# A decoder layer on one core: eighteen seven-product blocks in the up projection in place of sixteen

## Chip, cores and metric

The kernel runs on one core of a Trainium2 chip. The metric is the device time of one execution in microseconds, the median of several runs. Beside it stands the profile of one execution, with the start and length of every instruction on the engines PE (matmul), DVE (vector), ACT (scalar), POOL and SP (here mainly a DMA queue).

## The reference, cut to what matters

The layer has a mixer (two kinds of heads), a gated MLP with a causal convolution, and a gated table lookup projection. The change touches the first product of the MLP alone:

```python
h = rms_norm(x, ffn_norm_g[i])
u = h @ w_up[i]                       # (256, 2048) @ (2048, 11264), float32
a, g = jnp.split(u, 2, axis=-1)
a = causal_dwconv(a, conv_w[i], conv_b[i])
x = x + (jax.nn.gelu(a, approximate=False) * g) @ w_down[i]
```

There are 256 tokens, that is two row halves of 128.

## The kernel before, in words

**A float32 product in three.** Every operand is split into a high part (ACT casts it, line 1219, or 286 in the earlier stages) and a low part (DVE subtracts the high part from the raw value, line 1221 or 288). One product of 128 x 128 by 128 x 512 is three matmuls (`three`, lines 353 to 355): high by high, high by low, and low by high. The first of them needs the cast of the weights alone, the second needs the subtraction too.

**Column groups.** The up projection runs over 11 column groups (`up_group(q)`, q from 0 to 10). A group takes 512 columns of `a` and 512 of `g`, and the 2048 input rows as 16 slabs of 128. Its four accumulators (two row halves by two column halves, named `up00` to `up11`) fill four PSUM banks.

**Units.** A group is a list of units, each with at most two weight slabs to load, a split (cast and subtractions) and its matmuls. A plain unit (`p`) loads one slab of 128 x 1024 values (512 KB) and makes its four products, 12 matmuls. A *seven* treats two slabs as a 2 x 2 block product and makes it with seven products, as Strassen and Winograd do: 21 matmuls where two plain units make 24. It is four units in a row (`split1`/`fn1` to `split4`/`fn4`): its first unit loads both slabs and splits half of one; the third adds halves of the slabs on DVE (lines 1666 and 1667) before its split; the fourth does so too (lines 1677 and 1678). Four of the seven products go to banks of their own (`upP1`, `upP5`, `upP6`, `upP7`), which are the four banks that the accumulators of the next group will use; after the last seven of a group they are combined into `z_up` (ACT line 1688, DVE lines 1689 to 1691).

**The order table.** `ORDERS[q]` is a string with one letter for each unit: `p` a plain unit, `a` the next quarter of the first seven, `b` of the second. A group with one seven has 18 units, one with two has 20. In the kernel before, group 0 has two; after it groups with one and with two follow in turn, and the last two groups have one each: 16 sevens.

**The turn of a group.** When a group's last slab is done, ACT takes its four accumulators out (`up_rows`, line 1077), DVE adds the `z_up` terms (line 1084, two instructions) and transposes blocks (line 191, two), and 16 small DMAs move the blocks into columns (line 197, ten on SP's queue and six on POOL's). These jobs are tied to the last unit of the group and the first of the next (`TURN_AT`). The convolution and the GELU of the group (`up_act`: ACT lines 1103, 1106 and 1113, DVE lines 1110 and 1116, split in lines 147 and 148) are tied to units 9 to 18 of the next group (`ACT_AT`, `START`). From group 2 on, DVE lines 453 to 457 and ACT line 456 make sums of the previous group's result for the down projection.

**Buffers.** The split parts live in eight buffers (`hi0` to `hi3`, `lo0` to `lo3`), two for a unit and one for the first unit of a seven; a split runs at most four units ahead (`AHEAD_UP`). The raw slabs go into eight more spaces: `raw0` to `raw2`, two in each of the tiles `u32r` and `u36r`, and one in `xs`. SP's queue issues the loads in order, and the moves of a turn stand in the same queue.

**What sets the order.** The lines above say what depends on what; a scheduler then writes one fixed list of instructions for each engine. Each engine works its list in order.

The names `part<u>_0` and `part<u>_1` are the cast and the subtraction of unit u. With the change a unit's number rises by two behind each group that gains a seven; groups, not unit numbers, are compared below.

Of the kernel before, what the change touches and what calls it, by code (L numbers as in the profile page):

```python
# [43 lines left out]

FRONT = (8, 4, 4)
SEVENS_UP = 2
ORDERS = ("pppppp" "apapapap" "bpbbbp",
          *("pppppp" "apapapap" "pppp", "ppp" "apapapap" "bpbpbpb" "pp") * 4,
          *("pppppp" "apapapap" "pppp",) * 2)
START = [sum(map(len, ORDERS[:q])) for q in range(12)]  # L50
TURN_AT = (-1, -1, 0, 0)
GATE_ORDER = "ppppp" "apapapap" "bpbpbb" "p"
# [4 lines left out]
def layer_kernel(  # L57
# [954 lines left out]
    with tc.tile_pool(name="ffn", bufs=1) as fp:  # L1012
# [609 lines left out]
        def up_group(q):  # L1622
# [3 lines left out]

            n7 = "a" in ORDERS[q], "b" in ORDERS[q]
            first, n7 = 2 * sum(n7), sum(n7)
# [81 lines left out]
            kinds = {"p": iter(us), "a": iter(seven(0)), "b": iter(seven(1))}  # L1710
            return [next(kinds[c]) for c in ORDERS[q]]

# [71 lines left out]
```

## Time and profile before

| | |
|---|---|
| median of 3 runs (lowest, highest) | 1234.77 us (1232.65, 1235.25) |
| the profiled execution's own time | 1232.94 us |
| its span, first to last instruction | 1231.2 us |
| mixer and output projection | about 0 to 430 us of the span |
| up projection, 11 groups | about 430 to 905 us |
| down projection | about 905 to 1110 us |
| gate and output | about 1110 to 1231 us |
| DMA packets of the whole span | 276.36 MB, mean 224 GB/s |

A view of groups has one row for each line, engine and shape, with the count, the busy time and the mean length of one. A view of windows has one row for each stretch, and for each engine its busy time and number of instructions. A timeline has one row for instructions that follow each other, with start, length, engine, line and count; in square brackets stands the idle time before it and what ended it. The length of an instruction is longer than the distance to the next on the same engine, since they overlap a little: distances come from the timeline, not from the mean length. "us to landing" is the time from a DMA's issue to its end.

### The profile page before, as it was taken

The page shows a single profiled execution, that of the slowest core. Times are in us where ns is not written, and L with a number is a line of the kernel's source. Part 1 is how long each engine was busy: PE and PEld are TensorE (multiplying, and loading weights), DVE is VectorE, ACT ScalarE, POOL GpSimd, SP SyncE. Part 2 cuts the span into 40 slices and gives each one's busy share as a digit, 9 for nine tenths or more (in the row PEclk, how much of TensorE's full clock was granted, in tenths as well). Part 3 has the DMA queues.
Part 4 walks back from the last instruction along what each step waited for, and adds up shares of the span by engine and source line. Part 5 has one row for each costly group of instructions (what it writes and reads, how often), then busy time and mean ns, then how long its engine had stood idle before and what let it go on. Part 6 is the DMA issues. An engine that isn't in the chain of part 4 may idle for free.

```text
span 1231.2 us, 16367 instructions
## 1 busy us (share of the span) xinstructions
PE 1224.2 (99%) x5596; PEld 1031.2 (84%) x5596; DVE 978.5 (79%) x1210; ACT 747.8 (61%) x1095; POOL 186.8 (15%) x347
## 2 busy tenths in 40 slices
PE   9999999999999999999999999999999999999998
PEld 7999988888888888888888888888888888888887
DVE  6788857665565689789998898998788998899773
ACT  7667545565554455766676676757656556556552
POOL 2011237243304201011101101110110000050000
PEclk9999999999999999999999999999999999999999
DMA  8566687676557786777687678766797896777670
GB/s 304 181 198 195 175 229 223 185 221 188 161 183 218 224 312 208 241 218 242 204 273 242 183 255 268 225 174 221 240 316 247 298 345 208 253 230 229 199 230 35
DMA packets 131301, 276.36 MB, mean 224 GB/s; under 512 B 14906, under 2 KB 24626, under 8 KB 131090
## 3 DMA queue, kind: packets, MB, share of 16 engines
q1 hardware_dynamic: 119312, 256.87, 65.6%
q0 software_dynamic: 11520, 18.29, 5.3%
q8 instruction: 44, 0.72, 0.2%
q14 instruction: 40, 0.32, 0.1%
q10 hardware_dynamic: 385, 0.16, 0.0%
HBM read 247.46 MB, written 8.93 MB: 208 GB/s over the span
## 4 chain that ended last, share of the span: by engine, by line
PE 99%; DVE 0%; DMA 0%; ACT 0%; issue 0%; SPq 0%; DVEq 0%
PE up L353 11%; PE up L355 11%; PE up L354 11%; PE tg L343 9%; PE tg L344 9%; PE tg L342 8%; PE pg L353 3%; PE pg L354 3%; PE pg L355 3%; PE dnP L1271 1%; PE dnP L1270 1%; PE upP L355 1%; PE upP L354 1%; PE upP L353 1%; PE dnP L1269 1%; PE gt L354 1%
## 5 line engine op out<-in xcount | busy, mean ns | idle before, releaser
L288 DVE TENSOR_TENSOR lo<-raw,hi 128x1024 fp32r<-128x1024 f32 (+3 forms) x130 | 153.4, 1182 | 108.3 <-ACT hi L286 108.0
L355 PE MATMUL up<-part,x2T 128*128 128x512 f32 x608 | 236.6, 389 | 0.0
L354 PE MATMUL up<-part,x2T 128*128 128x512 f32 x608 | 236.5, 389 | 0.0
L1219 ACT CAST part<-raw 128x1024 fp32r<-128x1024 f32 (+1 forms) x147 | 146.5, 1007 | 111.5 <-PE up L355 35.1
L286 ACT CAST hi<-raw 128x1024 fp32r<-128x1024 f32 (+3 forms) x130 | 132.1, 1017 | 124.1 <-PE tg L344 70.1
L1221 DVE TENSOR_TENSOR part<-raw,part 128x1024 fp32r<-128x1024 f32 (+1 forms) x141 | 163.1, 1162 | 31.6 <-ACT part L1219 25.8
L353 PE MATMUL up<-part,x2T 128*128 128x512 f32 x608 | 185.0, 389 | 0.0
L354 PEld LDWEIGHTS up<-part,x2T 128*128 128x128 f32 x608 | 114.2, 188 | 23.6
L355 PEld LDWEIGHTS up<-part,x2T 128*128 128x128 f32 x608 | 114.1, 188 | 23.6
L353 PEld LDWEIGHTS up<-part,x2T 128*128 128x128 f32 x608 | 114.2, 188 | 23.6
L344 PE MATMUL tg<-hi,hT 128*128 128x512 f32 x288 | 113.7, 396 | 0.0
L343 PE MATMUL tg<-lo,hT 128*128 128x512 f32 x288 | 113.2, 393 | 0.2 <-DVE lo L288 0.2
L342 PE MATMUL tg<-hi,hT 128*128 128x512 f32 x288 | 112.5, 397 | 0.0
L197 POOL DMA_DIRECT2D EZ<-Y x66 | 35.0, 538 | 373.2 <-issue 205.3
L1219 ACT CAST part<-u36r 128x1024 fp32r<-128x1024 f32 (+1 forms) x46 | 47.8, 1041 | 35.1 <-PE up L355 16.3
L1221 DVE TENSOR_TENSOR part<-u36r,part 128x1024 fp32r<-128x1024 f32 (+1 forms) x46 | 55.5, 1207 | 11.5 <-ACT part L1219 7.2
L343 PEld LDWEIGHTS tg<-lo,hT 128*128 128x128 f32 x288 | 54.1, 188 | 11.3 <-DVE lo L288 0.4
L344 PEld LDWEIGHTS tg<-hi,hT 128*128 128x128 f32 x288 | 54.0, 188 | 11.2 <-DVE hT L151 0.2
L342 PEld LDWEIGHTS tg<-hi,hT 128*128 128x128 f32 x288 | 53.8, 188 | 10.6
L1221 DVE TENSOR_TENSOR part<-u32r,part 128x1024 fp32r<-128x1024 f32 (+1 forms) x44 | 50.3, 1145 | 12.1 <-ACT part L1219 9.2
L1219 ACT CAST part<-u32r 128x1024 fp32r<-128x1024 f32 (+1 forms) x44 | 43.4, 991 | 21.4 <-DVE u32r L1667 7.7
L354 PE MATMUL pg<-lo,hT 128*128 128x430 f32 (+1 forms) x156 | 55.7, 357 | 0.0
(861 smaller groups left out, 2714.3 us busy)
## 6 DMA issues: line engine op xcount, KB each, us to landing
raw<-in_w_up_dram SPq DMA_DIRECT2D x78, 512.0 KB, 5.1
raw<-in_w_in_dram SPq DMA_DIRECT2D x71, 512.0 KB, 4.3
u36r<-in_w_up_dram SPq DMA_DIRECT2D x43, 512.0 KB, 5.0
raw<-in_w_down_dram SPq DMA_DIRECT2D x42, 512.0 KB, 6.0
u32r<-in_w_up_dram SPq DMA_DIRECT2D x34, 512.0 KB, 5.2
raw<-in_w_out_dram SPq DMA_DIRECT2D x32, 512.0 KB, 4.8
xs<-in_w_up_dram SPq DMA_DIRECT2D x21, 512.0 KB, 4.9
w2b<-in_w_down_dram SPq DMA_DIRECT2D x20, 512.0 KB, 6.0
```

Of the source, the lines that this page charges most:

```text
L197: (other if other and (4 * a + b) % 3 else pool).dma_start(out=c[32 * b : 32 * b + 32, a::4], in_=y[32 * a : 32 * a + 32, :, b])
L286: act.copy(hi, raw)
L288: dve.tensor_sub(lo, raw, f32(hi))
L342: pe.matmul(o, ah, hi[:, i, :], start=first, stop=False)
L343: pe.matmul(o, ah, lo[:, i, :], start=False, stop=False)
L344: pe.matmul(o, al, hi[:, i, :], start=False, stop=last)
L353: pe.matmul(o, ah, hi, start=start, stop=False)
L354: pe.matmul(o, ah, lo, start=False, stop=False)
L355: pe.matmul(o, al, hi, start=False, stop=stop)
L1219: act.copy(r32(hi), raw)
L1221: dve.tensor_sub(r32(lo), raw, hi)
L1269: pe.matmul(o, ah, hi, start=first, stop=False)
```

## The change

The order table is written with two names, one for a group with one seven and one for a group with two, and the groups behind group 0 now follow as two, two, one, three times, and one at the end.

```diff
 FRONT = (8, 4, 4)
 SEVENS_UP = 2
-ORDERS = ("pppppp" "apapapap" "bpbbbp",
-          *("pppppp" "apapapap" "pppp", "ppp" "apapapap" "bpbpbpb" "pp") * 4,
-          *("pppppp" "apapapap" "pppp",) * 2)
+ONE = "pppppp" "apapapap" "pppp"
+TWO = "ppp" "apapapap" "bpbpbpb" "pp"
+ORDERS = ("pppppp" "apapapap" "bpbbbp", TWO, TWO, ONE, TWO, TWO, ONE, TWO, TWO, ONE, ONE)
 START = [sum(map(len, ORDERS[:q])) for q in range(12)]
```

Groups 1, 5 and 7 gain a seven, and group 6 loses one. Groups 1, 2, 5 and 8 now follow a group with two sevens with two of their own; before, no group did.

**ACT at the turn from group 0 to group 1.** Unit 23 was a plain unit and is now the first quarter of a seven (with half a slab to cast), and unit 24, a plain unit, has its slab in `u32r`. Before:

```order
L1077 ACTIVATE EZ_4102<-up11_4137,rstd_ffn_4098 128x512
L1219 CAST part22_0_4439<-u36r_4095 128x1024
L1077 ACTIVATE EZ_4102<-up10_4135,rstd_ffn_4098 128x512
L1219 CAST part23_0_4462<-u32r_4094 128x1024
L1219 CAST part24_0_4501<-raw24_0_4384 128x1024
```

Now:

```order
L1077 ACTIVATE EZ_4102<-up11_4137,rstd_ffn_4098 128x512
L1219 CAST part22_0_4437<-u36r_4095 128x1024
L1219 CAST part24_0_4499<-u32r_4094 128x1024
L1077 ACTIVATE EZ_4102<-up10_4135,rstd_ffn_4098 128x512
L1219 CAST part23_0_4462<-u32r_4094 128x512
```

The cast of unit 24 has moved ahead of the last of the four evictions (line 1077) and of the cast of unit 23.

**DVE at the turn from group 4 to group 5.** Group 5 begins with unit 96 before and with unit 98 now; it has one seven before and two now. Before:

```order
L1691 TENSOR_TENSOR xs_84<-upP5_5642,xs_84 128x2x512
L1221 TENSOR_TENSOR part99_1_5863<-u32r_4094,part99_0_5862 128x1024
L455 TENSOR_TENSOR Sf_5831<-xs_84,Sf_5831 128x128
L1084 SCALAR_TENSOR_TENSOR EZ_4102<-xs_84,rstd_ffn_4098,EZ_4102 128x1024 x2
L457 TENSOR_TENSOR Sp_5832<-Sf_5831,Sp_5832 128x4x128
L191 STREAM_TRANSPOSE Y_4103<-EZ_4102 128x8x4x32 x2
L1221 TENSOR_TENSOR part100_1_5902<-u32r_4094,part100_0_5901 128x1024
```

Now:

```order
L1691 TENSOR_TENSOR xs_84<-upP5_5648,xs_84 128x2x512
L455 TENSOR_TENSOR Sf_5836<-xs_84,Sf_5836 128x128
L1221 TENSOR_TENSOR part101_0_5869<-u36r_4095,part101_0_5869 128x512
L1084 SCALAR_TENSOR_TENSOR EZ_4102<-xs_84,rstd_ffn_4098,EZ_4102 128x1024 x2
L1666 TENSOR_TENSOR u36r_4095<-u36r_4095 128x512
L457 TENSOR_TENSOR Sp_5837<-Sf_5836,Sp_5837 128x4x128
L191 STREAM_TRANSPOSE Y_4103<-EZ_4102 128x8x4x32 x2
L1667 TENSOR_TENSOR u36r_4095<-u36r_4095 128x512
L1221 TENSOR_TENSOR part102_1_5907<-raw102_0_5757,part102_0_5906 128x1024
```

A subtraction of 1024 values has become one of 512, and the two additions of a seven (lines 1666 and 1667) now stand among the turn's instructions, ahead of the next full subtraction.

**PE at the same turn.** Unit 102 is now the fourth unit of its group, and unit 105 the third quarter of its first seven. Before, where the first row shown is 38 matmuls behind the start of group 5:

```order
L355 MATMUL up11_5870<-part98_0_5839,x2T0_3674 128x512
L353 MATMUL up11_5870<-part99_0_5862,x2T0_3674 128x512
L354 MATMUL up00_5867<-part99_1_5863,x2T0_3674 128x512
L355 MATMUL up00_5867<-part99_0_5862,x2T0_3674 128x512
L354 MATMUL up01_5869<-part99_1_5863,x2T0_3674 128x512
L355 MATMUL up01_5869<-part99_0_5862,x2T0_3674 128x512
```

Now, where it is 41 behind:

```order
L355 MATMUL upP1_5946<-part101_0_5869,x2T0_3674 128x512
L353 MATMUL up11_5875<-part102_0_5906,x2T0_3674 128x512
L353 MATMUL upP5_6004<-part105_0_5950,S_up0_4092 128x512
L353 MATMUL upP7_6008<-part105_0_5950,S_up0_4092 128x512
L354 MATMUL up00_5872<-part102_1_5907,x2T0_3674 128x512
L355 MATMUL up00_5872<-part102_0_5906,x2T0_3674 128x512
```

Two matmuls of unit 105, which read its cast, now stand ahead of the matmuls of unit 102 that read its subtraction. PE's list has the same form at the turn from group 0 to group 1, where the two matmuls read `part27_0` and stand 50 matmuls behind the start of group 1 (43 at the turn shown here); at the turns from group 1 to 2 and from 7 to 8 no matmul of a later unit stands there.

## The prediction

> **What bounds the kernel now.** I read the page first, its share of busy time and its chain of waits, then the view of who waited for whom, then windows that cut the up projection at the first matmul of its groups.
>
> ```profile
> span 1231.2 us, 16367 instructions
> ...
> PE 1224.2 (99%) x5596; PEld 1031.2 (84%) x5596; DVE 978.5 (79%) x1210; ACT 747.8 (61%) x1095; POOL 186.8 (15%) x347
> ...
> PEclk9999999999999999999999999999999999999999
> ...
> PE 99%; DVE 0%; DMA 0%; ACT 0%; issue 0%; SPq 0%; DVEq 0%
> ```
>
> The chain that ended last is PE's from end to end. The view of waits, asked for PE alone, has three rows, and all of them lie in the first stage:
>
> ```profile
> PE xT L159 <- DMA xs<-in_x_dram: 1.5, 1, 1.5
> PE warm L100 <- DVE ones L96: 1.1, 1, 1.1
> PE tg L343 <- DVE lo L288: 0.2, 1, 0.2
> ```
>
> So PE never stood still in the up projection, and a matmul that is left out there is worth its full time, as long as no wait comes up. The windows below are groups 4 (two sevens), 5 (one seven) and 2 to 9 together; the columns are PE, PEld, DVE, ACT and POOL with busy time and count, then the granted clock, the share of DMA, and GB/s.
>
> ```profile
> 600.84:643.00 42.16, 42.16 (x187) 34.92 (x186) 39.22 (x44) 30.34 (x43) 3.75 (x7) 1.00 0.75 236
> 643.00:685.84 42.84, 42.84 (x190) 35.48 (x189) 36.94 (x37) 27.51 (x38) 3.77 (x7) 1.00 0.76 236
> 515.84:855.84 340.00, 340.00 (x1501) 281.63 (x1500) 304.02 (x317) 231.22 (x313) 29.41 (x55) 1.00 0.73 228
> ```
>
> The last row gives PE's pace: 340.00 / 1501 = 0.2265 us for a matmul of 128x512. The first two give the worth of a seven: 42.84 - 42.16 = 0.68 us, three matmuls. They show its price too: DVE is busy for 39.22 of 42.16 us in a group with two sevens, and for 36.94 of 42.84 with one. A group of two has some 3 us to spare on DVE, and these are not spread evenly: at the turn of a group a run of evictions and transposes stands in DVE's list.
>
> **What goes away.** Three groups gain a seven and one loses one, two more in all, six matmuls fewer: 6 x 0.2265 = **-1.36 us**. The loads stay (a seven reads the slabs of two plain units). DVE and ACT get more work, but over the eight groups in the last window DVE is busy for 304.02 of 340 us, so what two sevens add is hidden in sum. What counts are the four turns at which a group of two now follows a group of two: 0 to 1, 1 to 2, 4 to 5 and 7 to 8.
>
> **The turn from group 4 to 5.** Up to here DVE's list is unchanged in kind, so the trace can be used with its own clock. Group 5 starts at 643.00, and this is the turn on DVE, on ACT and on PE (three answers of the timeline):
>
> ```profile
> 644.12 1.22 DVE L1691 TENSOR_TENSOR xs<-upP,xs 128x1024 f32<-128x1024 f32 x1
> 645.25 1.22 DVE L1221 TENSOR_TENSOR part<-u32r,part 128x1024 fp32r<-128x1024 f32 x1
> 646.38 0.28 DVE L455 TENSOR_TENSOR Sf<-xs,Sf 128x128 f32<-128x128 f32 x1
> 646.59 2.48 DVE L1084 SCALAR_TENSOR_TENSOR EZ<-xs,rstd_ffn,EZ 128x1024 f32<-128x1024 f32 x2
> 648.98 0.68 DVE L457 TENSOR_TENSOR Sp<-Sf,Sp 128x512 fp32r<-128x512 f32 x1
> 649.58 2.37 DVE L191 STREAM_TRANSPOSE Y<-EZ 128x1024 f32<-128x1024 f32 x2
> 651.87 1.18 DVE L1221 TENSOR_TENSOR part<-u32r,part 128x1024 fp32r<-128x1024 f32 x1
> ```
>
> ```profile
> 641.84 2.42 ACT L1077 ACTIVATE EZ<-up,rstd_ffn 128x512 f32<-128x512 f32 x4 [0.30 <-PE up L355]
> ...
> 650.72 1.05 ACT L1219 CAST part<-u32r 128x1024 fp32r<-128x1024 f32 x1 [3.40 <-DMA u32r<-in_w_up_dram]
> ```
>
> ```profile
> 643.00 0.39 PE L353 MATMUL up<-part,x2T 128*128 128x512 f32 x1
> ...
> 652.75 0.39 PE L355 MATMUL up<-part,x2T 128*128 128x512 f32 x1
> ```
>
> DVE has no idle time in it. From start to start an instruction of 1024 values takes 1.13 us (644.12 to 645.25), one of 512 takes 0.60 (648.98 to 649.58), the pair of line 1084 2.39 and that of line 191 2.29. In the new list the subtraction of 1024 is one of 512, and the additions of the seven come in, line 1666 ahead of the transposes and line 1667 behind them. From 645.25 on: 0.21 (L455) + 0.60 (subtraction) + 2.39 + 0.60 (L1666) + 0.60 (L457) + 2.29 = 651.94, so line 1667 ends at 651.94 + 0.68 = 652.62. Only then can ACT cast the third quarter of the seven, unit 105: 1.05 us (the ACT row), with 0.08 for the hand-overs, 653.8. In PE's list two matmuls that read this cast stand 43 matmuls behind the start of the group: 643.00 + 43 x 0.2265 = 652.74. **PE waits 1.1 us there.** The subtraction of unit 102, next on DVE, ends at 652.54 + 1.22 = 653.76, ahead of its matmul two places on, so it adds nothing. Everything behind these two matmuls waits with them.
>
> A PE that let a ready matmul pass a waiting one could take four matmuls of units 103 and 104 that read casts alone, 4 x 0.2265 = 0.9 us, and would wait only 0.2 here. The Trainium skill says that it does not (TensorE: Matmul & The Clock Gate, Step-by-step: what each phase is for): only weight loads are pulled ahead, and matmuls stay in program order. By that rule the 1.1 us stand; by the other the sum below would be 0.9 us less at each of two turns. No row here shows a waiting matmul in the up projection, so none can tell.
>
> **The turn from group 0 to 1.** Here the same form stands in PE's list, 50 matmuls behind the start of group 1, and something comes on top. The rows are those of DVE and ACT, the first matmul of group 1, SP's queue, and from the page the loads into `u32r` with their median time to landing:
>
> ```profile
> 474.98 1.22 DVE L1691 TENSOR_TENSOR xs<-upP,xs 128x1024 f32<-128x1024 f32 x1
> 476.11 1.22 DVE L1221 TENSOR_TENSOR part<-u32r,part 128x1024 fp32r<-128x1024 f32 x1
> 477.24 2.47 DVE L1084 SCALAR_TENSOR_TENSOR EZ<-xs,rstd_ffn,EZ 128x1024 f32<-128x1024 f32 x2
> 479.63 2.36 DVE L191 STREAM_TRANSPOSE Y<-EZ 128x1024 f32<-128x1024 f32 x2
> 481.92 1.18 DVE L1221 TENSOR_TENSOR part<-raw,part 128x1024 fp32r<-128x1024 f32 x1
> ```
>
> ```profile
> 472.75 1.05 ACT L1219 CAST part<-u36r 128x1024 fp32r<-128x1024 f32 x1
> 473.71 0.68 ACT L1077 ACTIVATE EZ<-up,rstd_ffn 128x512 f32<-128x512 f32 x1
> 474.28 1.04 ACT L1219 CAST part<-u32r 128x1024 fp32r<-128x1024 f32 x1
> ```
>
> ```profile
> 471.41 0.39 PE L353 MATMUL up<-part,x2T 128*128 128x512 f32 x1
> ```
>
> ```profile
> 469.92 0.54 SPq L1196 DMA_DIRECT2D u32r<-in_w_up_dram  x1
> ...
> 482.02 6.53 SPq L197 DMA_DIRECT2D EZ<-Y  x10
> 488.65 0.60 SPq L1196 DMA_DIRECT2D raw<-in_w_up_dram  x1
> ```
>
> ```profile
> u32r<-in_w_up_dram SPq DMA_DIRECT2D x34, 512.0 KB, 5.2
> ```
>
> With everything at hand DVE would run 476.11 + 0.60 (subtraction of 512) + 2.39 + 0.60 + 2.29 = 481.99, line 1667 would end at 482.68 and the cast of unit 27 at 483.8; PE needs it at 471.41 + 50 x 0.2265 = 482.74: 1.1 us again. But ACT's list now has the cast of unit 24 ahead of the last eviction (line 1077). Its slab goes to the space that this load at 469.92 fills, and by the median of its kind lands 5.2 us later, at 475.1. Behind the waiting cast stand that eviction and the cast of unit 23, and for these waits DVE: cast from 475.1, eviction from 476.1, cast of unit 23 from 476.6 to 477.3 (steps of 0.96 and 0.57 from the ACT rows, 0.6 for the half). DVE's subtraction starts at 477.3, not at 476.1, and all behind it moves by 1.2. **PE waits 2.3 us.** If the slab is early the wait is 1.1; if the scheduler's lists hide both, nothing. I take 2.3.
>
> **The other two turns.** At 1 to 2 no matmul is pulled ahead in this way. PE needs the subtraction of unit 44, 43 matmuls (9.74 us) behind the start of group 2. Ahead of it stand neither lines 455 and 457 nor line 1667: from the start of line 1691 it ends 1.13 + 2.39 + 0.60 + 2.29 + 0.60 + 1.22 = 8.23 later. If that line starts 1.12 behind the group's start, as at 643.00, the end is at 9.35, 0.4 ahead of need. At 7 to 8 line 1667 stands behind two more subtractions, and the same count comes out 0.8 ahead. I take 0 for both; the bounds are -0 and 1.1 each, the size found at 4 to 5.
>
> **The sum.** -1.36 + 1.1 + 2.3 + 0 + 0 = **+2.0 us**. The profiled execution took 1232.94 us (span 1231.2 and 1.7 around it), so it would take 1234.9. It lies 1.83 below the median 1234.77 of three runs whose spread is 2.6, so against that median: **1236.8 us**, +0.16%.
>
> **Rivals.**
>
> *A: the waits are covered.* Buffers or a shorter landing let ACT and DVE be a microsecond earlier, and PE does not wait: 1234.77 - 1.36 = 1233.4. For it: none of PE's waits lies in the up projection now. Against: DVE's seven rows at 644.12 have no gap, so there is nothing to gain there.
>
> *B: all four turns wait.* The margins of 0.4 and 0.8 at 1 to 2 and 7 to 8 are smaller than one DVE instruction. If DVE comes to line 1691 one instruction (1.13 us) late, PE waits there as well. This decides once DVE's spare time in a group of two, 42.16 - 39.22 = 2.9 us, is used up by the group before. Price: 1.1 each, +4.2 in sum, 1239.0: slower.
>
> *C: slabs late behind the moves.* The ten moves of a turn hold SP's queue (6.53 us at 482.02), and in a group of two that follows one of two the slab of its 13th unit is the first behind them, where before it was the 15th. At group 1 it would be issued at 488.7 and land 5.2 later, at 493.9; cast and subtraction (1.05 and 1.22) end at 496.2, and PE needs the subtraction 119 matmuls behind the group's start, at 498.4. A landing takes 2.2 us more than the median to be felt; then 1 us at each of four turns: 1240.8.
>
> *D: the clock falls.* A wait of 2.3 us is longer than any now (the longest is the 1.5 above, and the page's clock row stays at 9s). Were PE to run at half pace for as long as such a turn lasts, 643.00 to 652.75, that costs 9.75 / 2 = 4.9 us: 1241.7. The Trainium skill (TensorE: Matmul & The Clock Gate, What you observe and What's actually happening) puts the idle window at about 3.4 us, so by the Trainium skill a dip would cost about 1.7 us, an estimate, and a wait of 2.3 would not set it off by itself.
>
> **Chances.** The sum above 0.48, A 0.17, B 0.24, C 0.05, D 0.03, something unnamed 0.03. The likeliest alone gives 1235.4 to 1238.0 (2.3 or 1.1 at the first turn, 0.8 to 1.4 at the other). The range for 8 in 10 goes from just below A to above B: 1233.2 to 1240.5. A measurement here tells some 0.2%, 2.5 us, from no change. Faster by more than that: all six matmuls give but 0.11%, so only the unnamed, 0.03. Slower: B, C, D and the upper quarter of the likeliest, 0.32 + 0.13 = 0.45. The same: 0.52.
>
> **What would show it.** PE's waits should have rows with line 353 in the up projection: about 2 us at one place near 483 us, about 1 us near 655, released by ACT's cast (line 1219), and nothing else over 0.5 us. Six matmuls fewer on PE. On ACT a cast from `u32r` that waited for its DMA near 475. If there is no PE row at all, A is right; if rows near 525 and 780 as well, B; a release by a DMA, C; a granted clock under 1.00 in a group, D. The forecast is wrong as a whole if the time went into the down projection, where this page sees no change.

## The result, and the profile after

The changed kernel is slower: 1239.40 us in the median of 5 runs (1238.97 to 1239.44) against 1234.65 for the kernel before on the same chip (5 runs), a ratio of 1.0048 (95% interval 1.0037 to 1.0059), or 4.75 us. The forecast was 2.0. The profiled execution took 1238.97 us. From the page, span, PE's busy time and the granted clock in 40 slices:

```profile
span 1237.3 us, 16366 instructions
...
PE 1226.4 (99%) x5590; PEld 1030.9 (83%) x5590; DVE 986.5 (80%) x1222; ACT 751.1 (61%) x1099; POOL 186.8 (15%) x347
...
PEclk9999999999999999999999999999999999999999
```

Six matmuls are gone (5596 to 5590), and yet PE is busy for 2.2 us more: at a full-speed pace it would be 1.36 less. Where the time went is told by the first and the last matmul of the up projection, in the timelines of the kernel before and of the changed one:

```profile
429.91 0.39 PE L353 MATMUL up<-part,x2T 128*128 128x512 f32 x1
...
898.45 0.39 PE L355 MATMUL up<-part,x2T 128*128 128x512 f32 x1
```

```profile
429.93 0.39 PE L353 MATMUL up<-part,x2T 128*128 128x512 f32 x1
...
904.48 0.39 PE L355 MATMUL up<-part,x2T 128*128 128x512 f32 x1
```

Between them lie 468.54 us before and 474.55 now, 6.01 more; what comes ahead and behind is the same to 0.02. This length, free of what happens in the first stage, is the measure for most of what follows. PE's waits now have rows in the up projection (engine, line, what it waited for; total, times, longest):

```profile
PE upP L353 <- ACT part L1219: 3.3, 2, 2.1
...
PE up L353 <- ACT part L1219: 0.4, 1, 0.4
PE up L354 <- DVE part L1221: 0.4, 1, 0.4
```

These are four places. In PE's timeline a row in brackets gives the wait, and the distance of two rows the pace:

```profile
482.54 0.39 PE L353 MATMUL up<-part,x2T 128*128 128x512 f32 x1
485.02 0.73 PE L353 MATMUL upP<-part,S_up 128*128 128x512 f32 x2 [2.09 <-ACT part L1219]
...
486.18 0.63 PE L354 MATMUL up<-part,x2T 128*128 128x512 f32 x1
486.61 0.63 PE L355 MATMUL up<-part,x2T 128*128 128x512 f32 x1
...
655.90 0.39 PE L353 MATMUL up<-part,x2T 128*128 128x512 f32 x1
657.46 0.73 PE L353 MATMUL upP<-part,S_up 128*128 128x512 f32 x2 [1.17 <-ACT part L1219]
...
785.35 0.50 PE L354 MATMUL up<-part,x2T 128*128 128x512 f32 x1 [0.43 <-DVE part L1221]
...
893.32 1.20 PE L353 MATMUL up<-part,x2T 128*128 128x512 f32 x4 [0.44 <-ACT part L1219]
```

The first two are the waits at the turns 0 to 1 and 4 to 5. The third is at the turn 7 to 8, the fourth in the last group. Behind the first wait the matmuls stand 0.43 us apart (486.18 to 486.61) where 0.2265 is normal, and the window from there to 489.3 (columns PE, PEld, DVE, ACT, POOL, granted clock, share of DMA, GB/s) has the clock at 0.60:

```profile
485.00:489.30 4.30, 4.28 (x12) 3.38 (x13) 3.98 (x4) 0.28 (x1) 2.12 (x5) 0.60 0.73 186
```

Twelve matmuls in 4.28 us at 0.2265 would be 2.72: the low clock cost some 1.6 us of this execution.

**What the engines behind PE did.** DVE and ACT at the turn 0 to 1 of the changed kernel:

```profile
477.29 0.69 DVE L1221 TENSOR_TENSOR part<-u32r,part 128x512 fp32r<-128x512 f32 x1 [1.08 <-ACT part L1219]
477.90 2.48 DVE L1084 SCALAR_TENSOR_TENSOR EZ<-xs,rstd_ffn,EZ 128x1024 f32<-128x1024 f32 x2
480.29 0.68 DVE L1666 TENSOR_TENSOR u32r<-u32r 128x512 f32<-128x512 f32 x1
480.89 2.37 DVE L191 STREAM_TRANSPOSE Y<-EZ 128x1024 f32<-128x1024 f32 x2
483.18 0.65 DVE L1667 TENSOR_TENSOR u32r<-raw,u32r 128x512 f32<-128x512 f32 x1
```

```profile
475.12 1.05 ACT L1219 CAST part<-u32r 128x1024 fp32r<-128x1024 f32 x1 [1.30 <-DMA u32r<-in_w_up_dram]
...
483.92 1.04 ACT L1219 CAST part<-u32r 128x1024 fp32r<-128x1024 f32 x1 [1.22 <-DVE u32r L1667]
```

This is the predicted chain: the slab of unit 24 lands at 475.1, its cast holds up the eviction and the cast of unit 23, DVE stands for 1.08, line 1667 ends behind the transposes at 483.8, ACT casts, and PE starts when the cast ends. At the turn 4 to 5, DVE's and ACT's rows are these:

```profile
649.14 0.69 DVE L1221 TENSOR_TENSOR part<-u36r,part 128x512 fp32r<-128x512 f32 x1 [0.21 <-ACT part L1219]
...
655.63 0.65 DVE L1667 TENSOR_TENSOR u36r<-u36r 128x512 f32<-128x512 f32 x1
```

```profile
656.37 1.04 ACT L1219 CAST part<-u36r 128x1024 fp32r<-128x1024 f32 x1 [0.30 <-DVE u36r L1667]
```

At the turn 7 to 8 PE waits for the subtraction of unit 160, a plain unit:

```profile
776.08 1.22 DVE L1691 TENSOR_TENSOR xs<-upP,xs 128x1024 f32<-128x1024 f32 x1
777.21 1.22 DVE L148 TENSOR_TENSOR uC<-xs,uC 128x1024 fp32r<-128x1024 f32 x1
...
784.07 1.23 DVE L1221 TENSOR_TENSOR part<-u36r,part 128x1024 fp32r<-128x1024 f32 x1
```

And in the last group it waits for the cast of unit 208. ACT's list has the cast of unit 209 (from `xs`) ahead of it, with two sets of lines 1103 and 1106 around that:

```profile
887.73 1.05 ACT L1219 CAST part<-raw 128x1024 fp32r<-128x1024 f32 x1 [2.23 <-DMA raw<-in_w_up_dram]
...
889.99 1.05 ACT L1219 CAST part<-xs 128x1024 fp32r<-128x1024 f32 x1
...
892.23 1.04 ACT L1219 CAST part<-raw 128x1024 fp32r<-128x1024 f32 x1
```

### The profile page after: what moved, and what is told of

Read it like the earlier page. It is cut to its first block, busy times and chain, and to the rows that moved or that the text cites. A ratio compares the mean times of both kernels' runs of the same rounds, so it can differ in the third digit from the quotient of the medians.

```text
span 1237.3 us, 16366 instructions
## 1 busy us (share of the span) xinstructions
PE 1226.4 (99%) x5590; PEld 1030.9 (83%) x5590; DVE 986.5 (80%) x1222; ACT 751.1 (61%) x1099; POOL 186.8 (15%) x347
## 4 chain that ended last, share of the span: by engine, by line
PE 97%; DVE 1%; DMA 1%; ACT 1%; issue 0%; SPq 0%; DVEq 0%; ACTq 0%
PE up L354 11%; PE up L355 11%; PE up L353 11%; PE tg L343 8%; PE tg L342 8%; PE tg L344 8%; PE pg L353 3%; PE pg L354 3%; PE pg L355 3%; PE upP L353 1%; PE upP L355 1%; PE upP L354 1%; PE dnP L1270 1%; PE dnP L1269 1%; PE dnP L1271 1%; PE gt L353 1%
## 5 line engine op out<-in xcount | busy, mean ns | idle before, releaser
L354 PE MATMUL up<-part,x2T 128*128 128x512 f32 x596 | 232.9, 391 | 0.5 <-DVE part L1221 0.4
L355 PE MATMUL up<-part,x2T 128*128 128x512 f32 x596 | 232.9, 391 | 0.0
L353 PE MATMUL up<-part,x2T 128*128 128x512 f32 x596 | 181.8, 390 | 0.4 <-ACT part L1219 0.4
L354 PEld LDWEIGHTS up<-part,x2T 128*128 128x128 f32 x596 | 112.2, 188 | 24.6 <-DVE part L1221 1.4
L353 PEld LDWEIGHTS up<-part,x2T 128*128 128x128 f32 x596 | 112.0, 188 | 24.1 <-ACT part L1219 0.9
L355 PEld LDWEIGHTS up<-part,x2T 128*128 128x128 f32 x596 | 112.3, 188 | 23.4
L1219 ACT CAST part<-u36r 128x1024 fp32r<-128x1024 f32 (+1 forms) x51 | 51.0, 1000 | 35.6 <-PE up L354 9.8
L1221 DVE TENSOR_TENSOR part<-u36r,part 128x1024 fp32r<-128x1024 f32 (+1 forms) x51 | 59.0, 1159 | 15.6 <-ACT part L1219 10.9
```

Of the source, the lines that this page charges most:

```text
L353: pe.matmul(o, ah, hi, start=start, stop=False)
L354: pe.matmul(o, ah, lo, start=False, stop=False)
L355: pe.matmul(o, al, hi, start=False, stop=stop)
L1219: act.copy(r32(hi), raw)
L1221: dve.tensor_sub(r32(lo), raw, hi)
```

## The experiments

The time is the difference of the medians against the kernel before on the same chip, with the interval of the ratio; the length is that of the up projection in the profiled execution, less 468.54; the gaps are PE's waits in it of 0.2 us and more, by their place. (In the run with group 9 earlier one matmul of the down projection stands within that length; its 0.23 is taken off.)

| run | sevens | median, us | ratio, 95% | length | gaps at (us): size |
|---|---|---|---|---|---|
| changed kernel | 18 | +4.75 | 1.0037 to 1.0059 | +6.01 | 485: 2.09, 657: 1.17, 785: 0.43, 893: 0.44 |
| changed kernel, again | 18 | +4.71 | 1.0022 to 1.0047 | +4.29 | 486: 1.99, 657: 1.17, 785: 0.43, 893: 0.42 |
| changed kernel, third | 18 | +4.96 | 1.0023 to 1.0047 | +4.79 | 486: 1.98, 657: 1.18, 785: 0.43, 893: 0.64 |
| second seven in group 1 alone | 17 | +2.67 | 1.0008 to 1.0026 | +1.79 | 486: 2.05 |
| one seven in group 1 | 17 | +3.74 | 1.0020 to 1.0046 | +3.11 | 655: 1.17, 783: 0.43, 891: 0.97 |
| group 1 later | 18 | +3.48 | 1.0017 to 1.0040 | +3.54 | 526: 0.74, 655: 1.63, 783: 0.42, 891: 0.56 |
| group 5 earlier | 17 | +1.79 | 1.0010 to 1.0027 | +1.61 | 783: 0.43, 891: 0.20 |
| group 1 earlier | 18 | +3.13 | 1.0018 to 1.0036 | +3.57 | 484: 0.71, 655: 1.63, 784: 1.17 |
| best places, one in group 7 | 18 | +3.65 | 1.0018 to 1.0041 | +3.83 | 527: 0.73, 657: 0.27, 725: 0.37, 893: 0.64 |
| best places, groups as changed | 18 | +0.89 | 1.0000 to 1.0017 | +1.55 | 525: 0.73, 655: 0.28 |
| transposes four units later | 18 | +5.17 | 1.0030 to 1.0055 | +5.25 | 527: 1.22, 700: 1.13, 829: 1.13, 892: 0.26 |
| transposes twice at 0 to 1 | 18 | +6.05 | 1.0035 to 1.0060 | +6.04 | 486: 2.56, 530: 1.51, 658: 0.42, 787: 1.63 |
| transposes later, other groups | 18 | +6.84 | 1.0041 to 1.0068 | +7.14 | 527: 1.22, 572: 1.74, 617: 1.13, 746: 1.13 |
| the same, nineteen | 19 | +12.89 | 1.0093 to 1.0120 | +12.77 | 506: 0.20, 527: 1.23, 571: 1.74, 616: 1.74, 640: 0.21, 660: 0.70, 680: 0.79, 706: 1.75, 752: 1.13 |
| group 9 earlier | 18 | +3.84 | 1.0020 to 1.0045 | +3.99 | 485: 1.98, 656: 1.17, 784: 0.43, 847: 0.29 |
| waits taken off, eighteen | 18 | +2.93 | 1.0013 to 1.0032 | +3.25 | 526: 1.51, 680: 0.35, 808: 0.46 |
| waits taken off, seventeen | 17 | +0.82 | 0.9998 to 1.0016 | +0.55 | 636: 0.24 |

The two columns agree within 0.9 us, but for the first row (1.3), whose profiled execution has the low clock. So what these orders cost lies in the up projection, and PE's waits are nearly all of it.

**Half of the change at a time.** The first run has the kernel before with the second seven of group 1 alone, the second has the rest of the change:

```diff
-ORDERS = (..., TWO, TWO, ONE, TWO, TWO, ONE, TWO, TWO, ONE, ONE)
+ORDERS = (..., TWO, TWO, ONE, TWO, ONE, TWO, ONE, TWO, ONE, ONE)
```

> Seventeen sevens: the second seven of group 1 alone is added to the kernel before, so that only the turns 0 to 1 and 1 to 2 have two sevens on both sides. Theory (wait, then half clock): the wait of the changed kernel at 485 stays (its step is 2.48 us where 0.23 is normal: 2.25 more), and behind it the matmuls run at half pace for some 3.8 us as there (1.7 more); minus three matmuls, 0.68: the span is 3.3 us above the kernel before. Rival 1 (the low clock belongs to the whole of the change, not to this wait): the wait alone, 1.6 above, with no steps over 0.3 us behind it. Rival 2 (the waits of about 0.5 us in the last group are set by the number of sevens ahead): they are here at half their size. No wait near 528, the turn 1 to 2.

```diff
+ORDERS = (..., ONE, TWO, ONE, TWO, TWO, ONE, TWO, TWO, ONE, ONE)
```

> Seventeen sevens, with one seven in group 1: the other three gains and losses of the change stay. Theory: no wait near 485 and the clock is 1.00 in every window of the up projection; the wait at the turn 4 to 5 stays (1.4 us with its restart), that at 7 to 8 too (0.7), minus 0.68, so 1.4 us above the kernel before, and up to 2.3 if the small waits of the last group stay as well. Rival (the half clock comes with the turn of a group, whatever its wait): a window with a clock under 0.8 behind 655 too, 3 us above.

The wait at the turn 0 to 1 came alone, 2.05 us, with no low clock behind it: the length is 1.79 above, and 1.64 of it is the wait with its restart (2.32, see the account below) less the 0.68 of one seven. So the step that a gap of two microseconds brings the half clock fell at once (rival 1 gave 1.6). Rival 2 of the first run, the last group, is at zero rather than at half. The other half has the waits at 655 and 783 as in the changed kernel, and a larger one, 0.97, in the last group.

**The first seven of a group earlier or later.** `LATE` has four plain units ahead of the first seven and one behind the second, `EARLY` two and three, where `TWO` has three and two.

```diff
+LATE = "pppp" "apapapap" "bpbpbpb" "p"; EARLY = "pp" "apapapap" "bpbpbpb" "ppp"
+ORDERS = (..., LATE, TWO, ONE, TWO, TWO, ONE, TWO, TWO, ONE, ONE)
```

> The changed kernel with the first seven of group 1 one plain unit later (four plain units ahead of it, and one behind the second seven): nine matmuls, 2.04 us. Theory: the wait at 485 falls from 2.1 us to between 0 and 0.4, and the half pace behind it goes with it (1.7): 3.5 to 3.9 us below the changed kernel, some 1 us above the kernel before. Rival 1 (the half clock has another cause at that place, such as the loads or the moves): the clock still falls near 485, and only 2 us are saved. Rival 2 (with one plain unit behind the second seven, its sums are late at the next turn): a new wait near 528 of 1 to 2 us gives half of it back.

```diff
+ORDERS = (..., ONE, TWO, ONE, TWO, EARLY, ONE, TWO, TWO, ONE, ONE)
```

> As the run with one seven in group 1, and in group 5 the first seven one plain unit earlier, behind two: PE is at it nine matmuls, 2.04 us, sooner. Theory: the wait at the turn 4 to 5 grows from a gap of 1.2 us to 3.2, and now the clock falls to half behind it, as behind the gap of 2.1 at 485 of the changed kernel: 2.04 + 1.7 = 3.7 us above the run with one seven in group 1. Rival 1 (a gap at this place doesn't touch the clock, that at 485 had a cause of its own): 2.0 above, with the clock at 1.00. Rival 2 (the first seven's loads and sums are made earlier too, since DVE's list follows the order): less than 1 us above.

```diff
+ORDERS = (..., EARLY, TWO, ONE, TWO, TWO, ONE, TWO, TWO, ONE, ONE)
```

> The changed kernel with the first seven of group 1 one plain unit earlier (two plain units ahead of it, three behind the second seven). In group 5 this removed the wait, because line 1667 came ahead of the transposes in DVE's list. In group 1 it doesn't: line 1667 stands behind both transposes still, and one addition of a split further back, while PE is there nine matmuls, 2.04 us, sooner. Theory: the gap near 483 grows from 2.1 to between 4.1 and 5.3 us, and with it the clock falls for certain, to half for 3.8 us or more (1.7): 3.7 to 4.9 us above an execution of the changed kernel without the low clock. Rival (what counts is the place of the seven in the group, earlier is better): the gap is gone as it was in group 5, 2 us below.

Later in group 1: the wait at 485 is gone, and rival 2 is right on the place, if not on the size: 0.74 at the next turn, where 1 to 2 were forecast. The wait at 655 grew to 1.63, and it is there a wait of line 354 for a subtraction and no longer one of line 353 for a cast: an edit in group 1 changed the lists of group 5. Earlier in group 5: against the theory the wait all but vanished, 0.06 us. DVE's timeline of that run shows why:

```profile
648.56 2.47 DVE L1084 SCALAR_TENSOR_TENSOR EZ<-xs,rstd_ffn,EZ 128x1024 f32<-128x1024 f32 x2
650.95 0.68 DVE L1667 TENSOR_TENSOR u36r<-u32r,u36r 128x512 f32<-128x512 f32 x1
...
652.16 2.36 DVE L191 STREAM_TRANSPOSE Y<-EZ 128x1024 f32<-128x1024 f32 x2
```

Line 1667 now stands ahead of the transposes (2.3 us) and of line 457. In group 1 the same edit left it behind the transposes, and the gap still fell, to 0.71. The expectation there was wrong in its direction. What is left is another wait, of a plain unit's matmul for its subtraction:

```profile
483.63 0.50 PE L354 MATMUL up<-part,x2T 128*128 128x512 f32 x1 [0.71 <-DVE part L1221]
```

The wait for the seven's cast is gone, for two reasons. In PE's new list the two matmuls that read that cast stand 56 behind the start of the group and not 50, 1.36 us later, where the expectation had them 2.04 sooner. And from line 1691 to line 1667 there are 7.02 us,

```profile
474.77 1.22 DVE L1691 TENSOR_TENSOR xs<-upP,xs 128x1024 f32<-128x1024 f32 x1
...
481.79 0.65 DVE L1667 TENSOR_TENSOR u36r<-u32r,u36r 128x512 f32<-128x512 f32 x1
```

with no idle time between; in the changed kernel there are 8.18 (475.00 to 483.18) with the 1.08 that DVE stands for ACT. A cast from `u32r` stands ahead of the last eviction in this list too, but it starts at 474.00 without a wait for its slab, and the cast of the seven's first half slab is ahead of it. That is the term of 1.2 in the prediction, seen by its absence. The 1.36 and the 1.16 together are more than the 2.09 that PE waited for that cast.

**Is it the transposes ahead of line 1667?** Here the orders are those of the changed kernel, and at the turns 0 to 1, 4 to 5 and 7 to 8 the transposes are hung on later units:

```diff
-            for job, i in zip(up_turn(), TURN_AT if ...):
+            for job, i in zip(up_turn(), (-1, 3, 0, 4) if q in (0, 4, 7) else TURN_AT if ...):
```

> The groups of the changed kernel, but at the turns 0 to 1, 4 to 5 and 7 to 8 the two transposes of line 191 are hung on units 3 and 4 of the next group in place of the last unit and unit 0. In DVE's list line 1667 now stands ahead of both transposes at these turns. Theory (it is the turn's work ahead of the seven's half sums that PE waits for): the gaps at 485, 655 and 783 are gone, and no low clock in the up projection. In the last group ACT's list still casts unit 209 ahead of unit 208, as in the changed kernel, so the wait of 0.9 us near 890 stays: 0.9 - 1.36 = 0.4 us below the kernel before. Rival 1 (the moves, which follow the second transpose, come some four units later, 9 us, and what reads them or queues behind them is late): new waits in groups 1, 5 and 8, 1 to 3 us above. Rival 2 (ACT's cast of unit 24 ahead of unit 23 was the wait at 485): 2 us remain there.

DVE and ACT at the turn 0 to 1 of this run:

```profile
479.84 0.69 DVE L1666 TENSOR_TENSOR u32r<-u32r 128x512 f32<-128x512 f32 x1
480.56 0.69 DVE L1667 TENSOR_TENSOR u32r<-raw,u32r 128x512 f32<-128x512 f32 x1
...
484.58 1.24 DVE L191 STREAM_TRANSPOSE Y<-EZ 128x1024 f32<-128x1024 f32 x1
```

```profile
482.15 1.04 ACT L1219 CAST part<-u32r 128x1024 fp32r<-128x1024 f32 x1
```

Line 1667 runs 2.6 us sooner, and the waits at 485, 655 and 783 are all three gone. That settles what the waits are: the transposes stand ahead of what PE needs in DVE's list, of the seven's half sums at the first two turns and of a plain unit's subtraction at the third. At the turn 0 to 1 the slab of unit 24 is as late as before and DVE stands for the same 1.08; with line 1667 that much sooner, PE does not feel it. The kernel is no faster for it. Rival 1 is right: three new gaps of 1.13 to 1.22 stand at the next turns, 1 to 2, 5 to 6 and 8 to 9. At the first of them PE waits again for a cast behind line 1667, and the last piece of the GELU (line 1116) now stands between lines 1689 and 1691:

```profile
515.86 1.22 DVE L1116 TENSOR_TENSOR xs<-xs,EZ 128x1024 f32<-128x1024 f32 x1
...
524.60 0.68 DVE L1667 TENSOR_TENSOR u36r<-raw,u36r 128x512 f32<-128x512 f32 x1
```

```profile
527.11 0.73 PE L353 MATMUL upP<-part,S_up 128*128 128x512 f32 x2 [1.22 <-ACT part L1219]
```

In the changed kernel that piece ran at 513.30, ahead of line 1689 at 515.59. What was pushed back at one turn has come up at the next.

The opposite edit makes each transpose of the turn 0 to 1 twice (the values are the same; `twice` holds the turn 0 alone):

```diff
-                    square(y, t, 0, EZ[:, t])
+                    square(y, t, 0, EZ[:, t]); q in twice and square(y, t, 0, EZ[:, t])
```

> The changed kernel with each of the two transposes of line 191 at the turn 0 to 1 made twice (the second writes the same values). At that turn alone, line 1667 has two more transposes ahead of it in DVE's list, 2 x 1.15 = 2.3 us. Theory: the gap at 485 grows from 2.0 to 4.3 us, microsecond for microsecond, and the clock behind it falls for certain, since 4.3 us is longer than any gap that left it at 1.00 so far (2.05): 4.0 above an execution without the low clock, less 0.9, since in the last group ACT's list has its casts in order here. Rival 1 (the gap belongs to ACT's casts or to a load, not to DVE): the gap stays at 2.0. Rival 2 (no gap of such a size decides on the clock): the gap is 4.3 with steps of 0.23 us behind it, 1.7 less.

The expectation misread the list: of the four transposes only two stand ahead of line 1667, the others behind it, as DVE's rows at 485.60 and 487.87 show. So the run does not measure a transpose. The gap still grew by 0.47, and two rows tell from where:

```profile
475.83 1.05 ACT L1219 CAST part<-u32r 128x1024 fp32r<-128x1024 f32 x1 [1.76 <-DMA u32r<-in_w_up_dram]
...
478.01 0.69 DVE L1221 TENSOR_TENSOR part<-u32r,part 128x512 fp32r<-128x512 f32 x1 [1.55 <-ACT part L1219]
```

The slab of unit 24 kept ACT for 1.76 us here and for 1.30 in the first profile of the changed kernel; DVE stood 0.47 longer, and PE 0.47 longer. In the six profiles that have this order at the turn 0 to 1 (the changed kernel three times, the second seven in group 1 alone, group 9 earlier and this one) PE's gap is ACT's wait for that slab plus 0.79 to 0.80, from 1.18 and 1.98 to 1.76 and 2.56. So the late slab passes to PE in full: it is the prediction's term of 1.2, shown by its size.

The run also has the longest gap of the study:

```profile
485.74 0.73 PE L353 MATMUL upP<-part,S_up 128*128 128x512 f32 x2 [2.56 <-ACT part L1219]
```

```profile
485.74:490.00 4.26, 4.26 (x19) 3.53 (x20) 4.26 (x4) 1.06 (x1) 0.22 (x1) 1.00 0.41 123
```

Nineteen matmuls in 4.26 us, at a clock of 1.00: this gap was followed by no low clock.

**The low clock.** The changed kernel twice more:

> The changed kernel once more, with another profile. The run with the seven in group 1 alone had the same gap (2.05 us at 486, against 2.09) and no low clock behind it, so the theory that a gap of 2.1 us always halves the clock has fallen. Now: theory A (it is a matter of chance whether such a gap does it, so the executions lie in two clusters 1.7 us apart): the gaps at 485, 655, 783 and 891 as before, the up projection from its first to its last matmul 474.6 us long if the clock falls and 472.9 if not. Theory B (something else that only the full change has halves the clock): 474.6 again, with steps of 0.43 us behind 485.

> The changed kernel a third time, for the clock alone. So far the up projection has had gaps of 1.6 to 2.6 us in ten profiled executions, and half clock behind one of them (2.09), not behind 1.99, 2.05 or 2.56; at 7 us gaps of 1.62, 1.92 and 2.30 had it, and 1.54 and less did not. Theory A (chance, by where the gap falls in time): most likely none behind 485 again, up projection 472.8 us long, the median 4 to 5 us above the kernel before. Theory B (the changed kernel has it as a rule): steps of 0.43 us behind 485, 474.6 long.

Neither has it in the up projection. The window behind the wait of 1.99 us in the first of them:

```profile
485.97:489.80 3.83, 3.83 (x17) 3.14 (x18) 3.83 (x4) 1.05 (x1) 2.10 (x5) 1.00 0.75 193
```

The length without it is 4.29 and 4.79 above the kernel before, and the medians are still 4.71 and 4.96 above. So the low clock is not what makes the changed kernel slower. It does weigh in: of the 12 executions of these two runs, on one chip, 5 have a mean clock of 0.998, with a median of 1239.09 us, and the other 7 (0.999 or 1.000) one of 1237.71; of 42 executions of the kernel before beside them none has 0.998. Where the low clock fell is known for the three profiled executions of the changed kernel only: once at 485, twice at 7 us, in the first stage, which the change doesn't touch.

**The last group.** The last group's wait came in six kernels: the changed one, the runs with one seven in group 1, with group 1 later, with group 5 earlier, with the transposes four units later, and the next one here. In each of them ACT's list has the cast of the following unit ahead of the one that PE waits for; in all the others these casts are in order. The run with group 7 at one seven was meant to take the wait off, on the theory that it came with two there:

```diff
+ORDERS = (..., LATE, TWO, ONE, TWO, EARLY, EARLY, ONE, TWO, ONE, ONE)
```

> Eighteen sevens with each at the place that had the least wait so far: group 1 later by a plain unit, groups 5 and 6 earlier by one, one seven in group 7, so that the last four groups have 1, 2, 1, 1 as in the kernel before. Theory: no gap at 485 and 655, 0.7 us near 526 (as with the later seven alone), and none at 783 and 891, since these came with two sevens in group 7. With its restart that is 0.9 - 1.36 = 0.5 us below the kernel before; group 6 alone is unknown, 0 to 1.5 us of wait near 696, so between 0.5 below and 1 above. Rival (the waits of the last group come from the number of sevens, not from group 7): a gap of 0.5 to 1 us near 891 all the same.

It kept the wait (0.64), so that theory fell; and the next one, with two in group 7, has none. It is the best of the kernels with eighteen:

```diff
+ORDERS = (..., LATE, TWO, ONE, TWO, EARLY, ONE, TWO, EARLY, ONE, ONE)
```

> Eighteen sevens in the groups of the changed kernel, the first seven of group 1 one plain unit later, those of groups 5 and 8 one earlier. Theory: no gap at 485, 0.7 us near 526, less than 0.1 near 655 and, with line 1667 ahead of the second transpose there too, none near 783; the last group keeps 0.2 to 1 us. Sum: 0.9 + 0.3 + 0 + 0.4 to 1.2 - 1.36, so 0.2 to 1.0 us above the kernel before, in place of some 5. Rival (an earlier first seven at the turn 7 to 8 makes a wait as long as in the changed kernel, 0.4 us): 0.5 more.

To bring ACT's casts of the last group back into order, the one seven of group 9 was moved by a plain unit:

```diff
-ORDERS = (..., TWO, TWO, ONE, ONE)
+ORDERS = (..., TWO, TWO, "ppppp" "apapapap" "ppppp", ONE)
```

> The changed kernel with one edit in group 9: its one seven stands a plain unit earlier. By it the casts of units 208 and 209 come in order in ACT's list of the last group (they are swapped in all five kernels here that wait there, and in order in all that don't). Everything up to group 8 is as in the changed kernel. Theory: the gaps at 485, 655 and 783 are the same, those near 891 are gone: up projection 472.8 - 0.9 = 471.9 us, if the clock stays at 1.00. Rival 1 (the last group's loads are late behind the ten moves whatever ACT's order): 0.4 to 0.8 near 891 still. Rival 2 (the earlier seven of group 9 makes a wait of its own at the turn 8 to 9): a new gap near 825.

ACT's casts of units 208 and 209 in this run:

```profile
888.75 1.05 ACT L1219 CAST part<-raw 128x1024 fp32r<-128x1024 f32 x1 [0.94 <-DMA raw<-in_w_up_dram]
...
891.01 1.03 ACT L1219 CAST part<-xs 128x1024 fp32r<-128x1024 f32 x1
```

The casts are in order, and that of unit 208 starts at 888.75, when its slab lands, in place of 892.23. PE has no gap near 891. But the order of the casts is not all that changed. In the six kernels that wait, SP's list loads the slab of unit 208 behind that of unit 210, and PE's list has two pairs of units of the group's seven (203 and 204, 205 and 206) the other way round; in all the others both are in order. (With seventeen sevens each of these numbers is two less.) So this run does not part the casts from the loads. The traces do. In the changed kernel the slab of unit 208 was issued at 886.79 and landed at 891.20; a cast begun then would have ended at 892.25 (an estimate, with 1.05 for the cast), and PE came to its matmul at 892.88. ACT's list held the cast back to 892.23: there it is the order of the casts. The same sum comes out ahead of PE in four more of the six. In the run with one seven in group 1, whose wait of 0.97 is the longest, it does not, and the cast that PE waits for is this:

```profile
890.31 1.04 ACT L1219 CAST part<-raw 128x1024 fp32r<-128x1024 f32 x1 [0.16 <-DMA raw<-in_w_up_dram]
```

ACT stood ready and the slab was not there: that wait is the load's, and no order of the casts would have started it sooner. Rival 1, loads late behind the moves whatever ACT's order, did not come true in this run. Rival 2 is partly right: a gap of 0.29 came in at 847.

**Can more sevens pay?** With the transposes later at each turn between two groups of two:

```diff
+ORDERS = (..., TWO, TWO, TWO, ONE, TWO, TWO, ONE, TWO, ONE, ONE)
+            for job, i in zip(up_turn(), (-1, 3, 0, 4) if q in (0, 1, 2, 5) else TURN_AT if ...):
```

> Eighteen sevens: groups 0, 1, 2, 3, 5, 6 and 8 have two, the others one, and at each turn from two to two (0 to 1, 1 to 2, 2 to 3, 5 to 6) the transposes are hung on units 3 and 4 of the next group. The tail is that of the kernel before (1, 2, 1, 1), and ACT's list has the casts of the last group in order. Theory: no gap in the up projection but those under 0.1 us, and 1.36 us below the kernel before (its length 467.2 us in place of 468.5). Rival (the moves that come later with the transposes make what follows them late): 1 us or more of waits in groups 1, 2, 3 or 6, no gain.

```diff
+ORDERS = (..., TWO, TWO, TWO, TWO, TWO, TWO, ONE, TWO, ONE, ONE)
+            for job, i in zip(up_turn(), (-1, 3, 0, 4) if q in (0, 1, 2, 3, 4, 5) else TURN_AT if ...):
```

> As the run before with a nineteenth seven: groups 0 to 6 and 8 have two, with the transposes later at the six turns from two to two. Theory: DVE has the time (39 us of 42 in a group of two), so each seven is worth its three matmuls: 9 x 0.2265 = 2.04 us below the kernel before, the length of the up projection 466.5. Rival (with six groups of two on end DVE falls behind by a little in each, with no group of one to catch up): gaps that grow from turn to turn, 0.5 us or more at the last of them, and no more gain than with eighteen.

Both fell clearly, and the rivals were right that nothing is gained. With nineteen the gaps do not grow from turn to turn, though, as the rival has it (1.23, 1.74, 1.74, then 0.70 and 0.79, 1.75 and 1.13). PE's waits with nineteen:

```profile
PE upP L353 <- ACT part L1219: 7.6, 5, 1.7
PE up L353 <- ACT part L1219: 1.2, 3, 0.8
...
PE up L354 <- DVE part L1221: 0.7, 1, 0.7
```

At the turn 1 to 2 the gap is 1.22 or 1.23; at the turn 2 to 3, the third in a row with later transposes, it is 1.74. Last, two kernels in which the turn 0 to 1 alone is delayed, and by less:

```diff
+ORDERS = (..., TWO, TWO, ONE, TWO, EARLY, ONE, TWO, EARLY, ONE, ONE)
+            for job, i in zip(up_turn(), (-1, 1, 0, 1) if q in (0,) else TURN_AT if ...):
```

> Eighteen sevens in the groups of the changed kernel, the waits taken off one by one: at the turn 0 to 1 alone the transposes are hung one unit later (on units 1 and 1, not 3 and 4: line 1667 comes one place ahead of them), groups 5 and 8 have the first seven one plain unit earlier, and the last group's casts are in order. Theory: no gap at 485, under 0.3 near 655 and 783, none near 891; if the turn's work that comes two units later costs less at the next turn than the 1.2 us it did with units 3 and 4, 0 to 0.6 near 527: 0 to 1.0 - 1.36, so 0.4 to 1.4 us below the kernel before. Rival (any delay of the transposes comes back at the turn 1 to 2 in full): 1.2 there, no gain.

```diff
+ORDERS = (..., TWO, ONE, TWO, EARLY, ONE, TWO, ONE, TWO, ONE, ONE)
```

> Seventeen sevens: two in groups 0, 1, 3, 4, 6 and 8, one in the others; the transposes at the turn 0 to 1 one unit later, the first seven of group 4 one plain unit earlier. Theory: behind the turn 0 to 1 stands a group with one seven, which takes up the delay, so no gap near 527, and under 0.3 at the turn 3 to 4 near 612: 0.68 us below the kernel before, less 0 to 0.4. Rival (the delay makes a gap at the end of group 1 whatever follows): 1.2 near 527, 0.5 above.

With a group of two behind it, the delay came back in full, 1.51 at 526; with a group of one it did not come back. (With the longer delay of the run above it had, 1.13, also where a group of one follows.) But even there 1.1 us of small waits and steps over 0.24 us ate the 0.68 of the seventeenth seven. No run was faster than the kernel before.

## Why the prediction was wrong

**The two waits in the sum came as forecast; two more were put at nothing, and the sum was too small by half.** The terms, as measured in the second profile of the changed kernel, which has no low clock in the up projection. A wait is the step from the matmul ahead less 0.2265, with 0.11 more, since the second step behind each wait is 0.34.

| term | predicted | measured |
|---|---|---|
| six matmuls | -1.36 | -1.36 |
| turn 0 to 1 | +2.3 | +2.27 |
| turn 4 to 5 | +1.1 | +1.45 |
| turn 1 to 2 | 0 | 0 |
| turn 7 to 8 | 0 | +0.71 |
| last group | not in the sum | +1.04 |
| sum | +2.0 | +4.1, of 4.29 in the length |

**Six matmuls fewer:** right, 5596 to 5590.

**Turn 0 to 1:** right in place, cause and size. The cast of the slab started at 475.12 (475.1 forecast), DVE stood for 1.08 (1.2), line 1667 ended at 483.83. Its two parts are shown by runs: without the transposes ahead of line 1667 the wait is gone; where ACT's cast does not stand for its slab, that stretch of DVE is 1.16 shorter, and where it stood 0.47 longer PE's wait was 0.47 longer.

**Turn 4 to 5:** right in place and cause, 0.35 too small: DVE stood 0.21 for ACT's cast of the half slab, which the step took as "no idle time in it", and the restart of 0.11 was in no term. That PE kept its program order at a waiting matmul, as the Trainium skill has it (TensorE: Matmul & The Clock Gate, Step-by-step: what each phase is for), agrees with the trace: by the other rule 0.2 us were forecast there, and the wait was 1.17.

**Turn 7 to 8: this step failed.** "The same count comes out 0.8 ahead" was carried over from the turn 1 to 2 and not made from its own rows. There DVE has line 148 (1.13 us) and lines 454, 455 and 457 (1.0 together) behind line 1691, which the count left out, and one transpose fewer (1.16) ahead of the subtraction. From the start of line 1691 to the end of the subtraction are 9.22 us (776.08 to 785.30), where 8.23 were counted. PE came to its matmul 8.84 behind the start of line 1691, where the count leaves it some 9.0. So 0.8 ahead became 0.43 of a wait. Rival B had a wait at this turn, at 1.1 and with another cause, DVE an instruction late at line 1691; here the instructions behind that line made it. At the turn 1 to 2 B was wrong: the subtraction ended at 528.59, 0.3 ahead of its matmul (0.4 forecast).

**The last group: the larger failure.** The sum asked only at the four turns between groups of two. That a scheduler makes the lists anew, and that loads and casts could change places in group 10, two groups behind the last one it speaks of, was taken as nothing: "nothing else over 0.5 us". It cost 1.04, as much as the wait at 4 to 5 was thought to: two waits of 0.42 and 0.07 by PE's idle time, and the rest in the slower steps around them. By the landing of the slab it is the order on ACT that makes it there, and in the run with one seven in group 1 the load. Among the chances only "something unnamed", 0.03, has it.

**The clock.** Rival D had 0.03, on the rule of the Trainium skill (TensorE: Matmul & The Clock Gate, What's actually happening) that an idle window of some 3.4 us is needed. By that rule a wait of 2.3 would not set it off; the trace does not agree, since one of 2.09 did, in one of three profiles. The estimate of the cost that was worked out from that window of the Trainium skill, 1.7 us, fits the measured 1.6. As a part of the changed kernel's time it stands behind the waits: executions with a mean clock of 0.998 are 1.4 us longer than the others.

**The range** held the time, but the chances leaned to the wrong side: with the terms as they were measured the change is over the 0.2% at which a measurement tells it, and "the same" had 0.52. (A quarter of the likeliest's 0.48 is 0.12 and not the 0.13 that the chances count.) C was wrong: no wait of PE at these turns was released by a DMA. Where a late load did reach PE beyond the turn 0 to 1, it was in the last group.

## What to carry to other kernels

Where a scheduler writes fixed lists, compare the lists to their end, not only at the edited place: look for any instruction or load that has changed places with another whose result is needed sooner. A margin of under one instruction of the feeding engine is a chance of a wait and not a zero; each turn's count has to be made from that turn's own rows. And a wait that is removed by delaying other work on the same nearly full engine tends to come back at the next turn: here 1.1 to 1.7 us, and nothing of it only in the run where the delay was one or two units and a lighter group followed.

## What the runs showed of the hardware

**The clock falls behind some waits of 1.6 to 2.3 us and not behind others.** In all profiles the up projection had thirteen waits of 1.6 to 2.6 us, and one (2.09) was followed by a low clock; 1.98, 1.98, 1.99, 2.05 and 2.56, at the same place of the program, were not. At 7 us in the first stage PE's gaps of 1.62, 1.65, 1.92 and 2.30 us were followed by a low clock (0.67 from 6 to 10 us in the first of them), and those of 1.54 and less never. The Trainium skill (TensorE: Matmul & The Clock Gate, What's actually happening) says that the window by which the clock is set runs freely and does not start with the kernel. That would make it a matter of when the wait falls; the runs fit this and do not prove it.

**A restart costs a tenth of a microsecond.** Behind each of PE's 84 waits over 0.04 us in the up projection of the changed kernels, however short, the second matmul comes 0.33 to 0.34 us after the first and not 0.2265 (785.35 to 785.68 in the timeline of the changed kernel, for instance), so that five small waits cost half a microsecond more than their sum.
